# Output weights held for the second half, memory keys expanded once, unit products paced: a two-layer decoder trunk

## The chip, the cores and the metric

The kernel runs on one core of one Trainium2 chip, in one launch. The metric is the time of an execution on the device in microseconds (us). Three runs gave 2045.68, 2047.05 and 2050.27 us, so the median is 2047.05 us. The times were taken with random inputs of the sizes below.

## The reference

All is float32. The input x is 1024 tokens of width 1024. Layer 0 has a mixer of a recurrent block (width 768) beside four heads of attention over 256 memory rows, layer 1 one of sliding-window attention (12 query heads, 4 shared key/value heads, window 128) beside four heads over the same memory. After either mixer come one output projection and a SwiGLU network; each of these sits between two norms. Cut to what matters here:

```python
for l in range(2):
    hn = rms_norm(h, norm_mix_pre[l])
    mkv = rms_norm(mem, mem_norm) @ w_mem_kv[l]      # 4 heads of memory keys and values
    if l == 0:
        y = rg_lru(conv(x_r)) * gelu(gate)           # recurrent block
    else:
        y = sliding_window_attention_with_sinks(q, shared_k, shared_v, sinks)
    m_out = memory_attention(mq, mk, mv)
    mixed = concatenate([y, m_out]) @ w_out[l]       # the output projection, 1024 x 1024
    h = h + rms_norm(mixed, norm_mix_post[l])
    f = (silu(g) * u) @ w_ffn_out[l]                 # g, u = rms_norm(h, norm_ffn_pre[l]) @ w_ffn_in[l]
    h = h + rms_norm(f, norm_ffn_post[l])
```

## The kernel before, in words

Activations lie with the 1024 features on partitions, as 8 tiles of 128 (`KT`), and the tokens in two halves of 512 (`H`). Every float32 operand is split into a high and a low part (`split`, L87: a cast on ScalarE for the high one, L88, and a subtraction on VectorE for the low one, L89). A product is then three matmuls, low by high, high by high and high by low (`proj`, L148 to L150; names `al`, `ah` are the activation's parts, `wh`, `wl` the weight's). One output tile of 128 features for 512 tokens is 8 x 3 = 24 such matmuls, called a group here.

**The output projection** (`mix_out`) makes the 8 output tiles m0 to m7 for the first half, and then for the second. Its weights have two buffers (`wh`, `wl`, two of each, of 512 KB). In layer 0 the first half loads each weight, splits it, and stores m0 to m5 to DRAM (`keep`, `kept_wo`); m6 and m7 stay in the two buffers, and the second half begins with them and fetches m0 to m5 again (`fetch`, L191). In layer 1 all weights come from DRAM already split. Each output tile is copied from PSUM by ScalarE (L485) and squared and summed for the norm; for the last tile of a half the square (L490) goes by itself into `sq`. A matmul with `ones` (L233) sums `s` and `sq` over the partitions, and one with `ident` (L245) spreads the result.

**Layer 1's attention** is cut into 32 units, each a head for half the tokens: 4 memory heads (`mem_unit`, L378 to L399) and 12 window heads (`swa_unit`, L1063 to L1093) per half. A unit is a front part (scores on TensorE, maximum on VectorE, exponential on ScalarE, scaling on GpSimd) and a back part (transposes, casts, products with the values, and `acc`, L357). `attend` records the front of a unit and then the back of the one before it; it keeps the back's products in `outs`. The units are recorded between the 12 projection steps of each half (keys, values and six groups `wb`), by a table (`QUOTA`), and what is left of them between the output tiles of `mix_out`. There `place` fixes where the backs stand on TensorE: it makes the 48 matmuls that follow a chosen position wait in program order for a given product. A scheduler orders the rest within each engine. Each engine runs its instructions in that order, so one that waits holds all behind it.

The memory keys of layer 1 lie in DRAM (`kv1`). `mem_expand` splits them (`mkh`, `mkl`, L298 and L300), once for each of two pairs of heads in each half: four times in all. The loads, the stores and the fetches are issued on SyncE's queue.

Of the kernel before, what the change touches and what calls it, by code (L numbers as in the profile page):

```python
# [7 lines left out]
F32 = mybir.dt.float32  # L8
F32R = mybir.dt.float32r
# [4 lines left out]
P = 128  # L14
D = 1024
T = 1024
H = 512
KT = D // P
# [10 lines left out]
KSPLIT = 4  # L29
PLACED = 48  # L30
A_PLACES, F_PLACES, END_PLACES = (36, 54), (10, 20, 100, 110), (30, 48)
MIX_TAIL, MIX_PLACES = 2, (10, 20, 108, 118)
QUOTA = [0] * 8 + [1] * 4, [1] * 8 + [2] * 4
WEIGHT_LEAD, EVICT_LEAD, NORM_LEAD = 1000, 300, 300
NEXT_WEIGHTS = ([("wb", NL), ("wb", NL + 1), ("wk", 0), ("wk", 1), ("wv", 0), ("wv", 1)] +
                [("wb", j) for j in range(NL)] + [("wo", m) for m in range(KT)])
# [8 lines left out]
class Trunk:  # L45
# [39 lines left out]
        return self.tile(self.ap, 16, "ah", (P, H), F32R), self.tile(self.ap, 16, "al", (P, H), F32R)  # L85

    def split(self, hi, lo, src, eng=None):  # L87
        self.nc.scalar.copy(hi, src)  # L88
        return (eng or self.nc.vector).tensor_tensor(lo, src, hi.bitcast(F32), op=ALU.subtract)  # L89

    def table(self, *args, **kw):
# [389 lines left out]
    def mix_half(self, layer, act, order, steps, f, s):  # L481
        for i, (m, w) in steps:
            ps = self.proj(w(m), [act], 0, ks=order)
            f[m] = self.acc_tile()
            self.nc.scalar.copy(f[m], ps)  # L485
            if i < KT - 1:
                self.sumsq(s[0], f[m], i == 0)
            else:
                s.append(self.t("sq"))
                self.nc.scalar.activation(s[1], f[m], AF.Square)  # L490

    def mix_out(self, layer, y, order, src, early, ld):
        f, s, act = ([None] * KT, [None] * KT), [None, None], [None, None]
        hx = self.dp.tile([D, T], F32, name=f"hx{layer}")
        held, room = [], self.where["wh"][1]

        def new(m):
            if layer:
                w = self.fetch(("wo", m))
            else:  # L500
# [3 lines left out]
            held.append(w)  # L504
# [9 lines left out]
        a1 = [None] * KT  # L514
        s[0] = [self.t("s")]
        us = list(early)
        self.outs, self.mms = [], []
        for m in range(KT):
            for _ in range(-(-len(us) // max(KT - MIX_TAIL - m, 1))):
                self.attend(us.pop(0))  # L520
            if m == KT - MIX_TAIL:
                self.attend()
            done = [order[m]] if not early else order if m == KT - MIX_TAIL else []
            self.mix_split(y, 1, done, a1)
            self.mix_half(layer, a0, order, [(m, (m, new))], f[0], s[0])
        for i, g in enumerate(self.outs):
            self.place(self.mms, [[g]], [(i + 1) * len(self.mms) // (len(self.outs) + 1)])
        s[1] = [self.t("s")]
        steps = [(m, lambda m: held[m]) for m in range(KT - room, KT)]
        steps += [(m, lambda m: self.fetch(("wo", m))) for m in range(KT - room)]  # L530
        steps = list(enumerate(steps))
        self.mms = []
        self.mix_half(layer, a1, order, steps[:room], f[1], s[1])
        self.marks = []
        finish(0, self.rstd(s[0], "p")[1], ld, "s", "rsn")
        marks = self.marks
        self.mix_half(layer, a1, order, steps[room:], f[1], s[1])
# [225 lines left out]
    def ffn(self, layer, x, act, hx, finish, dst, final):  # L763
        nc = self.nc
# [97 lines left out]
        if not final:  # L862
            total(3, [(c12, c12)], ps)
            steps = order[5] + order[3]
            h0 = self.ffn_post(f0, rs, 0, gpost, r0, dst, [steps[12 * i] for i in POST_STEPS])
            for x, y in zip(c22, part):
                nc.vector.tensor_tensor(x, x, y, op=ALU.add)
            for i, g in zip(END_PLACES, marks):
                self.after(steps[i], g[-1])

            def fin():
                s = self.t("s")
                for k in range(KT):
                    self.sumsq(s, f1[k], k == 0, tag="sp")
# [47 lines left out]
    def run(self):  # L922
# [4 lines left out]
        common = dict(s=2, sq=1, sp=1, ld=2, rsn=2)  # L927
# [5 lines left out]
        self.phase("a", {"mm": 3, "gt": 2, "ss": 1, "tt": 1, "oo": 1}, mix_w, common, dict(rest=1),  # L933
                   dict(xr=4, graw=1, gwh=2, gwl=2, xc=2, xh=1, xl=1, gr=2, gi=2, a2=2), att)
        spare = [("xr", (P, 3 + H)), ("gr",), ("gi",), ("a2",)]
        mix = self.mix_out(0, *self.layer_a(), a["xT"], (), spare)
# [162 lines left out]
    def layer_b(self, h0, finish):  # L1099
# [3 lines left out]
        y = [[None] * KT for _ in range(2)]  # L1103
        kk = [[None] * 2 for _ in range(4)]
        vv = [None] * 8
        self.mem_tags = 0

        def half(n, act, f, w0, done):
            acts = [act, act]
            s = self.t("s")  # L1110
            take = self.sums([(nc.vector, s)], "00000000", ("sp", "sq"))
            for k in range(KT):
                take(k, f[k])
            rc = self.rcol(s, f"n{n}")
# [43 lines left out]
            for j in range(NL):  # L1158
                y[n][j] = self.acc_tile()
                self.rope(y[n][j], self.proj(self.fetch(("wb", j)), acts, n), tab)  # L1160
                done()

        def units(n):
            us, kv = [], {}

            def mem(j, e):
                if not kv:
                    kv["f"] = [self.load(d).rearrange("p (i c) -> p i c", i=2) for d in self.kv1]
                if e == 0:
                    kv[j] = self.mem_expand(kv["f"], j)  # L1170
                return self.mem_unit(y[n][NL + j], e, kv[j], y[n][NL + j])

            for j in range(2):
                for e in range(2):
                    us.append(lambda j=j, e=e: mem(j, e))
# [6 lines left out]
        def step(n):  # L1182
            us, at = units(n), [0]

            def done():
                i = at[0]
                at[0] += 1
                if n == 0 and i == 9:
                    h1.extend(finish())
                if i == 3:  # L1190
                    ready.extend(us[:4])
                elif i >= 6:
                    ready.extend(us[2 * i - 8:2 * i - 6])
                for _ in range(min(QUOTA[n][i], len(ready))):
# [77 lines left out]
```

## Time and profile before

| what | value |
|---|---|
| median of three runs | 2047.05 us |
| the profiled execution's own time | 2045.31 us |
| its span, from the first to the last instruction | 2043.5 us |
| outside of the span | 1.8 us |
| mean granted TensorE clock | 0.987 |
| TensorE busy | 1978.9 us, 97% of the span |
| VectorE, ScalarE, GpSimd busy | 1411.4, 1021.7, 479.2 us |

The table is read so: TensorE is busy in almost the whole span, and the other engines are not. The share hides three things, however. A matmul that runs at half clock counts as busy all the same; idle time on TensorE is spread over many short waits; and a matmul's end is modelled, so two that follow each other overlap in the rows. Waits are therefore read from the timeline, where a row that was waited for has the idle time before it and its releaser in brackets.

### The profile page before, as it was taken

The numbers are of one execution on the slowest core, as the hardware profiler recorded it, in microseconds if no ns is written. First come the engines' busy times: TensorE is split into PE (matmuls) and PEld (weight loads), VectorE is DVE, ScalarE is ACT, GpSimd is POOL, SyncE is SP. The second block draws the span as 40 slices with busy tenths as digits, with TensorE's granted clock in tenths as the row PEclk, the third lists the DMA queues.
The fourth block names the chain that finished last, engine by engine and source line by source line (L and its number), as shares of the span: only waits on it lengthen the run. The fifth ranks groups of instructions, "written<-read, shape, count | busy, mean of one in ns | idle before, by whom it ended". The sixth has DMA issues, their size and how long they took to land.

```text
span 2043.5 us, 27804 instructions
## 1 busy us (share of the span) xinstructions
PE 1978.9 (97%) x9368; PEld 1639.0 (80%) x9368; DVE 1411.4 (69%) x2313; ACT 1021.7 (50%) x1953; POOL 479.2 (23%) x476
## 2 busy tenths in 40 slices
PE   7999999999999999999999989999999999999997
PEld 6787877888888887888787877888888888888887
DVE  7877856787667676445878888678755655764566
ACT  6757774344444444445535677644433333344551
POOL 4323420014344231000034442200232323300001
PEclk9999999999999999999999989999999999999998
DMA  5422448137767879665545313171453453686653
GB/s 170 154 79 79 131 153 298 67 132 252 264 225 247 276 259 364 226 211 186 168 168 197 124 62 104 43 278 68 155 180 129 160 179 133 204 288 194 207 187 128
DMA packets 183552, 364.34 MB, mean 178 GB/s; under 512 B 20209, under 2 KB 25585, under 8 KB 183409
## 3 DMA queue, kind: packets, MB, share of 16 engines
q1 hardware_dynamic: 183408, 362.57, 52.7%
q8 instruction: 73, 1.20, 0.2%
q14 instruction: 71, 0.57, 0.1%
HBM read 254.48 MB, written 108.00 MB: 177 GB/s over the span
## 4 chain that ended last, share of the span: by engine, by line
PE 79%; DVE 9%; ACT 4%; issue 3%; DMA 3%; POOL 1%; SPq 0%; POOLq 0%; DVEq 0%; ACTq 0%
PE mm L622 12%; PE mm L624 12%; PE mm L623 12%; PE mm L730 6%; PE mm L731 6%; PE mm L732 6%; PE mm L148 5%; PE mm L149 5%; PE mm L150 5%; PE oo L1093 1%; PE tt L1086 1%; PE mm L601 1%; PE mm L602 1%; PE oo L233 1%; PE mm L603 1%
## 5 line engine op out<-in xcount | busy, mean ns | idle before, releaser
L88 ACT CAST ch<-wq 128x512 fp32r<-128x512 f32 x311 | 193.1, 621 | 423.0 <-PE mm L623 217.9
L89 DVE TENSOR_TENSOR cl<-wq,ch 128x512 fp32r<-128x512 f32 x311 | 230.7, 742 | 194.0 <-ACT ch L88 118.9
L148 PE MATMUL mm<-al,wh 128*128 128x512 f32 x616 | 250.8, 407 | 15.4 <-DVE al L965 7.4
L150 PE MATMUL mm<-ah,wl 128*128 128x512 f32 x616 | 248.3, 403 | 4.5 <-DVE wl L89 3.2
L622 PE MATMUL mm<-al,ch 128*128 128x512 f32 x640 | 252.4, 394 | 0.0
L624 PE MATMUL mm<-ah,cl 128*128 128x512 f32 x640 | 251.0, 392 | 0.0
L623 PE MATMUL mm<-ah,ch 128*128 128x512 f32 x640 | 250.3, 391 | 0.0
L149 PE MATMUL mm<-ah,wh 128*128 128x512 f32 x616 | 248.2, 403 | 0.0
L730 PE MATMUL mm<-tl,ch 128*128 128x512 f32 x532 | 207.7, 390 | 3.7 <-DVE tl L89 3.7
L731 PE MATMUL mm<-th,ch 128*128 128x512 f32 x532 | 207.0, 389 | 0.0
L732 PE MATMUL mm<-th,cl 128*128 128x512 f32 x532 | 205.1, 389 | 0.0
L622 PE MATMUL mm<-tl,ch 128*128 128x512 f32 x480 | 188.9, 393 | 0.9 <-DVE tl L89 0.9
L624 PE MATMUL mm<-th,cl 128*128 128x512 f32 x480 | 188.4, 393 | 0.0
L623 PE MATMUL mm<-th,ch 128*128 128x512 f32 x480 | 187.3, 390 | 0.0
L633 DVE TENSOR_TENSOR c<-c,mm 128x512 f32<-128x512 f32 x120 | 82.3, 686 | 110.7 <-PE mm L624 110.4
L148 PEld LDWEIGHTS mm<-al,wh 128*128 128x128 f32 x616 | 118.5, 192 | 43.9 <-DVE al L965 9.4
L150 PEld LDWEIGHTS mm<-ah,wl 128*128 128x128 f32 x616 | 118.6, 193 | 33.1 <-DVE wl L89 5.3
L624 PEld LDWEIGHTS mm<-ah,cl 128*128 128x128 f32 x640 | 120.1, 188 | 28.1
L623 PEld LDWEIGHTS mm<-ah,ch 128*128 128x128 f32 x640 | 120.2, 188 | 26.4
L622 PEld LDWEIGHTS mm<-al,ch 128*128 128x128 f32 x640 | 120.2, 188 | 26.0
L149 PEld LDWEIGHTS mm<-ah,wh 128*128 128x128 f32 x616 | 118.7, 193 | 23.1
L642 POOL TENSOR_TENSOR x<-wq,wq 128x512 f32<-128x512 f32 x36 | 50.1, 1391 | 329.6 <-DMA wq<-in_wi_dram 329.6
(347 smaller groups left out, 4300.1 us busy)
## 6 DMA issues: line engine op xcount, KB each, us to landing
wq<-in_wi_dram SPq DMA_DIRECT2D x168, 256.0 KB, 4.9
xz<-hd SPq DMA_DIRECT2D x154, 256.0 KB, 4.3
th<-xz SPq DMA_DIRECT2D x154, 256.0 KB, 3.6
wp<-in_wf_dram SPq DMA_DIRECT2D x112, 256.0 KB, 4.2
wz<-wp SPq DMA_DIRECT2D x88, 256.0 KB, 2.6
wq<-wz SPq DMA_DIRECT2D x56, 256.0 KB, 3.7
wraw<-in_wa_dram SPq DMA_DIRECT2D x27, 512.0 KB, 3.5
wq<-in_wf_dram SPq DMA_DIRECT2D x42, 256.0 KB, 3.8
```

What stands on the lines that cost most here:

```text
L88: self.nc.scalar.copy(hi, src)
L89: return (eng or self.nc.vector).tensor_tensor(lo, src, hi.bitcast(F32), op=ALU.subtract)
L148: self.mms += [nc.tensor.matmul(out, wh, al, start=i == 0, stop=False), nc.tensor.matmul(out, wh, ah, start=False, stop=False), nc.tensor. ...
L149: nc.tensor.matmul(out, wh, ah, start=False, stop=False),
L150: nc.tensor.matmul(out, wl, ah, start=False, stop=i == len(ks) - 1)]
L622: ins += [mm(out, wh, xl, start=start and k == 0, stop=False, skip_group_check=not start), mm(out, wh, xh, start=False, stop=False, skip_g ...
L623: mm(out, wh, xh, start=False, stop=False, skip_group_check=not start),
L624: mm(out, wl, xh, start=False, stop=k == 3, skip_group_check=not start)]
L633: add = lambda o, x, y: nc.vector.tensor_tensor(o, x, y, op=ALU.add)
L730: ins += [mm(ps[m], wh[:, m], xl[:, cs], start=start and p == 0, stop=False, skip_group_check=not start), mm(ps[m], wh[:, m], xh[:, cs], s ...
L731: mm(ps[m], wh[:, m], xh[:, cs], start=False, stop=False, skip_group_check=not start),
L732: mm(ps[m], wl[:, m], xh[:, cs], start=False, stop=p == NFB // 2 - 1, skip_group_check=not start)]
```

## The change

Five things are done, and TensorE's set of matmuls stays the same.

1. Layer 0 holds four output weights instead of two. m4 and m5 lie in the two buffers, m6 and m7 are split in halves straight into tiles of the attention (`SPARE`: `qs`, `pb`, `ph`). Only m0 to m3 go to DRAM; m2 and m3 come back in quarters of 256 KB into the same spare tiles. The second half uses m4, m5, m6, m7, m0, m1, m2, m3, with an order of contraction of its own (`LATE_ORDER`).
2. In layer 0 the casts of the second half's activations are recorded one by one, each after the copy of a tile (`self.after(self.cast, self.evict)`).
3. In both layers the second half's first 48 matmuls must follow the last one of the first half (`place(self.mms, [[last]], [0])`).
4. In layer 1 the memory keys are expanded once for both halves (`kv`), in other tiles (`kvf` in `pb`), and the second half's memory units stand between the window units (`MEM_UNITS`). The sums for the norms use one tile `sq` instead of `sp` and `sq`.
5. In layer 1 two more units lie before `mix_out` (`QUOTA`), and the last 22 backs (`PACED`) are spread evenly over the matmuls from step 5 of the second half on (`PACED_FROM`, `OUT_LAG`), instead of the last 12 over those of `mix_out` alone.

```diff
+PACED_FROM, PACED = 5, 22
+LATE_ORDER = [0, 1, 2, 3, 6, 7, 4, 5]
+SPARE = [[("qs", "qs"), ("pb", "pb")], [("pb", "pb"), ("ph", "ph")]]
-MIX_TAIL, MIX_PLACES = 2, (10, 20, 108, 118)
-QUOTA = [0] * 8 + [1] * 4, [1] * 8 + [2] * 4
+MIX_TAIL, OUT_LAG, MIX_PLACES = 2, 27, (10, 20, 108, 118)
+QUOTA, MEM_UNITS = ([0] * 8 + [1] * 4, [1] * 6 + [2] * 6), (2, 5, 8, 12)
...
-        held, room = [], self.where["wh"][1]
+        room = self.where["wh"][1] if layer else 2 + len(SPARE)
+        held = {}
...
+            else:
+                raw, w = self.t("wraw", (P, KT, P)), spare(m - KT)
+                nc.sync.dma_start(raw, self.a["wo"][layer, m])
+                for i in range(2):
+                    self.split(*w[i], raw[:, 4 * i:4 * i + 4])
...
+        def again(m):
+            if layer or m < len(SPARE):
+                return self.fetch(("wo", m))
+            w = spare(m - len(SPARE))
+            for i in range(2):
+                for x, d in zip(w[i], self.parted["wo", m]):
+                    nc.sync.dma_start(x.bitcast(F32), self.quad(d[:, i * H:i * H + H]))
...
-        self.outs, self.mms = [], []
+        if not layer:
+            self.outs, self.mms = [], []
...
-            done = [order[m]] if not early else order if m == KT - MIX_TAIL else []
-            self.mix_split(y, 1, done, a1)
+            if early and m == KT - MIX_TAIL:
+                self.mix_split(y, 1, order, a1)
             self.mix_half(layer, a0, order, [(m, (m, new))], f[0], s[0])
-        for i, g in enumerate(self.outs):
-            self.place(self.mms, [[g]], [(i + 1) * len(self.mms) // (len(self.outs) + 1)])
+            if not early:
+                self.mix_split(y, 1, [late[m]], a1)
+                if 0 < m < KT - 1:
+                    self.after(self.cast, self.evict)
+        outs = self.outs[-PACED:]
+        for i, g in enumerate(outs):
+            self.place(self.mms, [[g]], [OUT_LAG + (i + 1) * (len(self.mms) - OUT_LAG) // (len(outs) + 1)])
...
+        last = self.mms[-1]
         self.mms = []
...
+        self.place(self.mms, [[last]], [0])
...
-        self.mem_tags = 0
+        self.mem_tags = 1
...
-            us, kv = [], {}
+            us = []
...
-                    kv["f"] = [self.load(d).rearrange("p (i c) -> p i c", i=2) for d in self.kv1]
-                if e == 0:
-                    kv[j] = self.mem_expand(kv["f"], j)
+                    kv.update({i: self.mem_expand(kvf, i) for i in range(2)})
...
+                if n == 1 and i == PACED_FROM:
+                    self.mms = []
...
-                    ready.extend(us[:4])
+                    for j, u in enumerate(us[:4]):
+                        ready.insert(MEM_UNITS[j], u)
```

**TensorE at the end of layer 0's first half.** `mm_2851` and `mm_2849` are the group of m7 before and after, `mm_2881` and `mm_2883` the first group of the second half, `oo` the sums of the norm. Before:

```order
L148 MATMUL mm_2851<-al_2541,wh_2847 128x512
L149 MATMUL mm_2851<-ah_2540,wh_2847 128x512
L150 MATMUL mm_2851<-ah_2540,wl_2848 128x512
L233 MATMUL oo_2939<-ones,sq_2878 128x1 x4
L149 MATMUL mm_2881<-ah_2672,wh_2807 128x512
```

After:

```order
L151 MATMUL mm_2883<-al_2669,wh_2717 128x512
L152 MATMUL mm_2883<-ah_2668,wh_2717 128x512
L153 MATMUL mm_2883<-ah_2668,wl_2718 128x512
L151 MATMUL mm_2883<-al_2712,wh_2717 128x512
L236 MATMUL oo_3001<-ones,s_2544 128x1 x4
L236 MATMUL oo_3001<-ones,sq_2876 128x1 x4
L152 MATMUL mm_2883<-ah_2711,wh_2717 128x512
```

Before, the sum of `sq` stood right behind the last matmul of m7; after, ten matmuls of the next group stand between. In layer 1 the order there changes in the same way.

**ScalarE in the same place.** `ah` are the casts of the second half's activations, `wh` that of a weight, `acc` the copy of an output tile. Before:

```order
L356 COPY acc_1648<-oo_2504 64x512
L88 CAST ah_2586<-acc_1648 128x512
L88 CAST ah_2629<-acc_1715 128x512
L88 CAST ah_2672<-acc_1788 128x512
L88 CAST ah_2715<-acc_1942 128x512
L88 CAST ah_2758<-acc_2015 128x512
L88 CAST ah_2801<-acc_2203 128x512
L88 CAST ah_2841<-acc_2276 128x512
L88 CAST wh_2847<-wraw_2845 128x1024
L485 COPY acc_2796<-mm_2771 128x512
```

After:

```order
L488 COPY acc_2746<-mm_2721 128x512
L91 CAST ah_2751<-acc_1615 128x512
L211 ACTIVATE sq_2748<-acc_2746 128x512
L359 COPY acc_1648<-oo_2504 64x512
L488 COPY acc_2786<-mm_2761 128x512
L91 CAST ah_2791<-acc_1648 128x512
L211 ACTIVATE sq_2788<-acc_2786 128x512
L488 COPY acc_2830<-mm_2805 128x512
L91 CAST ah_2835<-acc_2203 128x512
L91 CAST ah_2878<-acc_2276 128x512
```

Seven casts stood in a row ahead of a weight's cast; now they stand singly behind copies, and no weight's cast is behind them.

**TensorE in layer 1's attention.** `mm_11906` (before) and `mm_11055` (after) are groups of the second half: `mm_11906` is the first output tile, `mm_11055` the query projection `wb1`; the rows between are products of units. Before, with the first and the last rows of a stretch of 144:

```order
L148 MATMUL mm_11906<-al_11756,wh_11902 128x512
L149 MATMUL mm_11906<-ah_11755,wh_11902 128x512
L150 MATMUL mm_11906<-ah_11755,wl_11903 128x512
L1063 MATMUL ss_11210<-kl_2068_9582,qs_11190 128x256
...
L393 MATMUL tt_11886<-ident,pb_11637 128x128 x2
L148 MATMUL mm_11906<-al_11760,wh_11902 128x512
```

After, with the first and the last rows of a stretch of 88:

```order
L151 MATMUL mm_11055<-al_10000,wh_11051 128x512
L1123 MATMUL oo_10876<-pl_10861,vv_2080_9626 128x256
...
L1123 MATMUL oo_11191<-ph_11184,vv_2086_9710 128x128
L152 MATMUL mm_11055<-ah_9999,wh_11051 128x512
```

Before, the stretch without a projection matmul held 166 matmuls of units; after, one of 103 stands earlier, and behind it 504 matmuls of units and 296 of projections alternate to the end of the first half of `mix_out`.

## Rows read from the trace of the kernel before

**Rows 1.** The page: busy time, and shares of the chain that ended last.

```profile
PE 1978.9 (97%) x9368; PEld 1639.0 (80%) x9368; DVE 1411.4 (69%) x2313; ACT 1021.7 (50%) x1953; POOL 479.2 (23%) x476
...
PE 79%; DVE 9%; ACT 4%; issue 3%; DMA 3%; POOL 1%; SPq 0%; POOLq 0%; DVEq 0%; ACTq 0%
```

**Rows 2.** Windows: us; busy of PE, PEld, DVE, ACT, POOL; clock; DMA share; GB/s.

```profile
450.00:475.00 25.00, 25.00 (x111) 20.42 (x110) 20.43 (x30) 10.15 (x18) 8.74 (x6) 1.00 0.80 282
...
306.40:309.80 3.40, 3.40 (x10) 2.67 (x9) 0.00 (x0) 0.00 (x0) 0.69 (x1) 0.50 0.00 0
330.30:337.10 6.80, 6.54 (x17) 4.88 (x18) 0.00 (x0) 1.93 (x4) 0.00 (x0) 0.50 1.04 396
```

**Rows 3.** Timeline of TensorE, layer 0's output projection: start, us, [idle before, releaser].

```profile
294.27 0.50 PE L148 MATMUL mm<-al,wh 128*128 128x512 f32 x1 [1.80 <-ACT wh L88]
...
304.74 1.05 PE L233 MATMUL oo<-ones,sq 128*128 128x1 f32 x8 [1.34 <-ACT sq L490]
...
330.56 0.77 PE L148 MATMUL mm<-al,wh 128*128 128x512 f32 x1 [2.35 <-DMA wh<-kept_wo]
...
347.53 0.47 PE L148 MATMUL mm<-al,wh 128*128 128x512 f32 x1 [0.69 <-ACT acc L485]
...
354.83 0.47 PE L148 MATMUL mm<-al,wh 128*128 128x512 f32 x1 [0.80 <-ACT ah L88]
...
362.02 0.51 PE L601 MATMUL mm<-al,th 128*128 128x512 f32 x1 [0.68 <-ACT acc L485]
```

**Rows 4.** Timeline of ScalarE, the same place.

```profile
289.52 3.75 ACT L88 CAST ah<-acc 128x512 fp32r<-128x512 f32 x7 [2.81 <-DVE acc L357]
293.17 1.04 ACT L88 CAST wh<-wraw 128x1024 fp32r<-128x1024 f32 x1
```

**Rows 5.** Timeline of SyncE's queue, the same place.

```profile
317.78 6.24 SPq L554 DMA_DIRECT2D hx<-acc  x8
324.11 0.54 SPq L191 DMA_DIRECT2D wh<-kept_wo  x1
```

**Rows 6.** Windows of layer 1's attention, second half, to the end of `mix_out`'s first half.

```profile
1158.70:1197.40 38.70, 38.70 (x234) 34.08 (x232) 31.61 (x86) 21.76 (x60) 20.19 (x27) 1.00 0.39 137
1197.40:1233.80 36.40, 28.65 (x153) 23.77 (x150) 31.97 (x80) 30.85 (x93) 13.84 (x29) 0.81 0.00 1
1233.80:1324.70 90.90, 88.31 (x528) 76.18 (x527) 66.32 (x189) 67.11 (x181) 24.05 (x48) 0.98 0.24 82
```

**Rows 7.** Windows inside the second of these.

```profile
1200.70:1207.50 6.80, 6.66 (x28) 5.52 (x28) 5.17 (x21) 5.43 (x17) 2.41 (x4) 0.50 0.00 0
...
1221.10:1224.50 3.40, 3.30 (x16) 3.24 (x16) 3.04 (x6) 2.08 (x9) 2.08 (x6) 0.51 0.00 0
```

**Rows 8.** Windows of L149 alone, a third of the projections' matmuls: PE, PEld.

```profile
1158.70:1197.40 38.70, 14.27 (x36) 6.61 (x35) 1.00 0.39 137
1197.40:1233.80 36.40, 0.00 (x0) 0.00 (x0) 0.81 0.00 1
1233.80:1324.70 90.90, 24.84 (x63) 11.90 (x63) 0.98 0.24 82
```

**Rows 9.** Windows of L357 alone, one for each unit's end: DVE.

```profile
1158.70:1197.40 38.70, 3.39 (x5) 1.00 0.39 137
1197.40:1233.80 36.40, 4.08 (x6) 0.81 0.00 1
1233.80:1324.70 90.90, 10.22 (x15) 0.98 0.24 82
```

**Rows 10.** Window before the shared keys' projection, where VectorE splits the memory queries.

```profile
1022.00:1036.00 14.00, 14.00 (x68) 11.70 (x67) 8.50 (x12) 3.68 (x6) 4.78 (x4) 1.00 0.11 47
```

**Rows 11.** Timeline of VectorE and TensorE at the second expansion of the keys.

```profile
1085.18 3.19 DVE L300 TENSOR_TENSOR mkl<-ld,mkh 64x256 fp32r<-64x256 f32 x4
...
1087.62 0.36 PE L378 MATMUL ss<-mkl,qs 128*128 128x256 f32 x1 [2.24 <-DVE mkl L300]
```

**Rows 12.** Timeline of TensorE, layer 1's end of the first half of `mix_out`.

```profile
1326.23 1.23 PE L233 MATMUL oo<-ones,sq 128*128 128x1 f32 x8 [0.55 <-ACT sq L490]
```

More of the change, by code (lines that the diff above doesn't have):

```diff
@@ L87, in split @@
     def split(self, hi, lo, src, eng=None):
-        self.nc.scalar.copy(hi, src)
+        self.cast = self.nc.scalar.copy(hi, src)
         return (eng or self.nc.vector).tensor_tensor(lo, src, hi.bitcast(F32), op=ALU.subtract)
@@ L484, in mix_half @@
             f[m] = self.acc_tile()
-            self.nc.scalar.copy(f[m], ps)
+            self.evict = self.nc.scalar.copy(f[m], ps)
             if i < KT - 1:
@@ L492, in mix_out @@
     def mix_out(self, layer, y, order, src, early, ld):
+        nc = self.nc
         f, s, act = ([None] * KT, [None] * KT), [None, None], [None, None]
         hx = self.dp.tile([D, T], F32, name=f"hx{layer}")
-        held, room = [], self.where["wh"][1]
+        room = self.where["wh"][1] if layer else 2 + len(SPARE)
+        held = {}
         def new(m):
@@ L499, in new @@
                 w = self.fetch(("wo", m))
-            else:
+            elif m < KT - len(SPARE):
                 w = self.weight(self.a["wo"][layer, m])
@@ L503, in new, with spare @@
                     self.keep(("wo", m), w)
-            held.append(w)
+            else:
[3 more added lines that the diff above has]
+                    self.split(*w[i], raw[:, 4 * i:4 * i + 4])
+            held[m] = w
+            return w
+        def spare(i):
+            return [[self.quad(self.t(tag, dt=F32R)) for tag in tags] for tags in SPARE[i]]
+        def again(m):
[5 more added lines that the diff above has]
+                    nc.sync.dma_start(x.bitcast(F32), self.quad(d[:, i * H:i * H + H]))
             return w
@@ L513, in mix_out @@
         a0 = self.mix_split(y, 0, order)
-        a1 = [None] * KT
+        a1, late = [None] * KT, order if layer else LATE_ORDER
         s[0] = [self.t("s")]
         us = list(early)
-        self.outs, self.mms = [], []
+        if not layer:
+            self.outs, self.mms = [], []
         for m in range(KT):
@@ L522, in mix_out @@
                 self.attend()
-            done = [order[m]] if not early else order if m == KT - MIX_TAIL else []
-            self.mix_split(y, 1, done, a1)
+            if early and m == KT - MIX_TAIL:
+                self.mix_split(y, 1, order, a1)
             self.mix_half(layer, a0, order, [(m, (m, new))], f[0], s[0])
-        for i, g in enumerate(self.outs):
-            self.place(self.mms, [[g]], [(i + 1) * len(self.mms) // (len(self.outs) + 1)])
+            if not early:
[5 more added lines that the diff above has]
+            self.place(self.mms, [[g]], [OUT_LAG + (i + 1) * (len(self.mms) - OUT_LAG) // (len(outs) + 1)])
         s[1] = [self.t("s")]
         steps = [(m, lambda m: held[m]) for m in range(KT - room, KT)]
-        steps += [(m, lambda m: self.fetch(("wo", m))) for m in range(KT - room)]
+        steps += [(m, again) for m in range(KT - room)]
         steps = list(enumerate(steps))
+        last = self.mms[-1]
         self.mms = []
-        self.mix_half(layer, a1, order, steps[:room], f[1], s[1])
+        self.mix_half(layer, a1, late, steps[:room], f[1], s[1])
         self.marks = []
@@ L536, in mix_out @@
         marks = self.marks
-        self.mix_half(layer, a1, order, steps[room:], f[1], s[1])
+        self.mix_half(layer, a1, late, steps[room:], f[1], s[1])
+        self.place(self.mms, [[last]], [0])
         for i, g in zip(MIX_PLACES, marks):
@@ L873, in fin @@
                 for k in range(KT):
-                    self.sumsq(s, f1[k], k == 0, tag="sp")
+                    self.sumsq(s, f1[k], k == 0)
                 rs1 = self.rstd(s, "p")[1]
@@ L926, in run @@
         self.kv1 = [self.dp.tile([P, H], F32, name=f"mkv1_{i}") for i in range(2)]
-        common = dict(s=2, sq=1, sp=1, ld=2, rsn=2)
+        common = dict(s=2, sq=1, rsn=2)
         att = dict(qs=2, pb=4, ph=2, pl=2, nm=6, sm=6, es=6)
@@ L932, in run @@
                dict(wq=6, wp=4), quad(2), quad(3), quad(1))
[L933 removed]
+        self.phase("a", {"mm": 3, "gt": 2, "ss": 1, "tt": 1, "oo": 1}, mix_w, {**common, "sp": 1}, dict(rest=1),
                    dict(xr=4, graw=1, gwh=2, gwl=2, xc=2, xh=1, xl=1, gr=2, gi=2, a2=2), att)
@@ L1110, in half @@
             s = self.t("s")
-            take = self.sums([(nc.vector, s)], "00000000", ("sp", "sq"))
+            take = self.sums([(nc.vector, s)], "00000000", ("sq",))
             for k in range(KT):
@@ L1161, in half @@
                 done()
+        kvf = [self.load(d, "pb").rearrange("p (i c) -> p i c", i=2) for d in self.kv1]
+        kv = {}
         def units(n):
-            us, kv = [], {}
+            us = []
             def mem(j, e):
                 if not kv:
-                    kv["f"] = [self.load(d).rearrange("p (i c) -> p i c", i=2) for d in self.kv1]
-                if e == 0:
-                    kv[j] = self.mem_expand(kv["f"], j)
+                    kv.update({i: self.mem_expand(kvf, i) for i in range(2)})
                 return self.mem_unit(y[n][NL + j], e, kv[j], y[n][NL + j])
```

## The prediction, made before the changed kernel ran

> **What bounds the kernel now.** I read the page first. TensorE is busy in 97% of the span and takes 79% of the chain that ended last; the next engine, VectorE, is at 69% and 9% [rows 1]. So the time is TensorE's. Its set of matmuls is the same after the change, and what can be won is only its idle time and the time at half clock.
>
> Next I read the windows, to see what a matmul costs when nothing is waited for. 111 matmuls of 512 columns fill 25.00 us, which is 0.225 us each [rows 2]. The small matmuls of the attention units have a price of their own. In the first window of [rows 6] TensorE has no idle time; of its 234 matmuls 36 x 3 = 108 are projections [rows 8], so the 126 of units took 38.7 - 108 x 0.225 = 14.4 us, 0.114 us each. (From the order I count 106 and 128, which gives 0.116; I use 0.113, the start-to-start distance that units show where they run on without a wait.)
>
> With these two prices the three windows of [rows 6] can be held against their contents. I count matmuls in the order, since a few records are missing from the trace. The first loses about 0.4 us. The second holds 166 matmuls of units and no projection [rows 8]: 36.4 us against 166 x 0.113 = 18.8, so 17.6 us are lost, and a matmul costs 0.219 us there. The third holds 338 of units and 190 of projections: 90.9 - 38.2 - 42.8 = 9.9 us lost. Together they lose 28 of 166.0 us. The second window shows why: without projections between, units wait for each other's steps on VectorE and ScalarE (31.97 and 30.85 us busy of 36.4), and the clock falls to a mean of 0.81 [rows 6].
>
> Last I read the timeline where the change acts. Layer 0's projection has single waits and two stretches at half clock [rows 2, 3]; layer 1 has a wait for memory keys and one at the end of `mix_out`'s first half [rows 11, 12].
>
> **The change part by part: layer 0.** All of these waits lie on TensorE, so each counts in full.
>
> - 1.80 us for a weight's cast [rows 3]. It stood behind seven casts in a row, which took 3.75 us [rows 4]. After the change no weight's cast is behind them: gone.
> - 1.34 us for the square of the last tile [rows 3], followed by 3.4 us at clock 0.50 [rows 2], which costs half of that, 1.7 us. Ten matmuls, 2.25 us, now stand between m7's last and the sums. The copy and the square were done 1.34 us after TensorE had come to them, so 2.25 us cover them.
> - 2.35 us for a weight that was fetched late [rows 3]. Its fetch was issued at 324.11, behind eight stores that had held the queue for 6.24 us [rows 5], and 6.4 us ahead of the matmul. The stretch at half clock behind it lasts 6.8 us [rows 2] and costs 3.4. With four weights held, the first fetched weight is needed 4 x 24 x 0.225 = 21.6 us after the half begins instead of 10.8, and 4 MB are fetched in place of 6 MB (each weight is two tensors of 512 KB). What is late next would be the fetch of m2 and m3 into the spare tiles, which waits for m6's and m7's last use, but these are needed four groups later, some 21 us, against the 6.4 us of [rows 5].
> - 0.69 and 0.80 us at the fifth and sixth fetched weights [rows 3] and two waits of about half a us behind them, 2.5 us in all. These weights were fetched into a buffer that was just released; the last two of the new order have been on the way for far longer.
>
> The sum is 1.80 + 3.04 + 5.75 + 2.47 = 13.1 us.
>
> Two costs come against it. The feed-forward network's first weights are kept in tiles that overlay the spare ones. So the casts of its first weights now wait for the last matmuls of m2 and m3, and ScalarE's later casts stand behind them in its queue. Before, this seam cost 0.68 us [rows 3]. I can't see the new wait in this trace. At the least it is nothing; at the most it is a whole chain of a cast, a subtraction and the evictions queued with them, some 10 us if everything that stood on ScalarE in the 3.75 us row [rows 4] came twice or more. I take 2.5 us, near the two waits of that row's kind (1.80 and 2.81), and 0.9 us more, half of a short half-clock stretch [rows 2], since long ones followed waits of 1.34 and 2.35 us. Layer 0 is then worth 13.1 - 3.4 = 9.7 us; from 13.1 down to 3.
>
> **Layer 1, the keys.** The wait of 2.24 us for `mkl` [rows 11] goes, and with it a stretch of 3.4 us at clock 0.50 behind it (three stretches of this length bear on the sum, and one of them stands in [rows 2]): 2.24 + 1.7 = 3.9 us. The two expansions move to where VectorE is busy for 8.50 of 14 us and TensorE has projections of its own [rows 10]; they cost about 3 us each on VectorE [rows 11] and fit, though the shared values behind them may come 0.5 us later. I take 3.4 us, from 1 to 3.9.
>
> **Layer 1, the end.** The ten matmuls cover the square here as well: 0.55 us [rows 12] and a half-clock stretch of 3.4 us, 1.7 us, together 2.2.
>
> **Layer 1, the pacing.** This is the largest term and the least certain. The stretch without a projection is not gone: the order leaves 103 matmuls of units alone, now ahead of the first paced position, at the second query projection. At the price of [rows 6] they lose 103 x (0.219 - 0.113) = 10.9 us instead of 17.6. Behind it 504 matmuls of units and 296 of projections alternate, 123.6 us by the two prices. Nothing lost in them would be like the first window of [rows 6], with 0.83 projections to a unit's matmul; 0.029 us lost at each unit's matmul, like the third, with 0.56, would be 14.8 us. The ratio here is 296 / 504 = 0.59, at the lower end, but the third window was unevenly filled. Another row gives a bound: in the second and the third window a unit ended every 36.4 / 6 = 6.07 and 90.9 / 15 = 6.06 us [rows 9], with and without projections. If that is the units' own pace, 21 paced ones take 127.3 us and 3.7 us are lost. I take 9 us, the middle of 3.7 and 14.8. The loss is 10.9 + 9 = 20 us instead of 28: 8 us gained, between 0 and 17 (14.8 lost and 2 of late first backs at one end, none at the other).
>
> The half clock is part of the price of those 103 matmuls. The row shows it at a mean of 0.81, though no wait in the window was longer than a wait that left the clock alone elsewhere (1.80 us at 294.27 [rows 3]); of the 36.4 us 13.6 were at 0.50, two of the three stretches are in [rows 7], and they cost 6.8 us. The Trainium skill has two rules for this. "TensorE: Matmul & The Clock Gate", section "HAM oscillation — how this bites in real kernels", has the clock fall after long waits for DMA between bursts; by that the new stretch keeps its clock and loses 103 x (29.6 / 166 - 0.113) = 6.7 us instead of 10.9, and the forecast would be 4 us lower. Its section "A second HAM failure mode: psum-queue depth-cycling" has frequent short waits do the same; by that the price stays. The trace agrees with the second, at 0.81.
>
> **The sum.** 9.7 + 3.4 + 2.2 + 8 = 23.3 us. From the profiled execution's 2045.31 us this gives 2022.0. The median of the runs shown is 1.7 us above that execution, so I predict 2024 us.
>
> **The rivals.**
>
> 1. The paced stretch runs as the first window of [rows 6], with nothing lost, and the seam in layer 0 costs nothing. Then layer 0 gives 13.1, the keys 3.9, the end 2.2, the pacing 28 - 10.9 = 17.1: 36.3 us, 2011 us. For it: an even ratio of projections, and VectorE needs only (31.61 + 31.97 + 66.32) / 26 = 5.0 us for a unit [rows 6, 9]. Against it: the pace of 6.07 us.
> 2. The loss only moves. The 103 matmuls and 14.8 us behind them leave the pacing a gain of 2.3, and the seam in layer 0 takes 10: 3.1 + 1 + 2.2 + 2.3 = 8.6 less some late backs, 2038 to 2043 us.
> 3. Slower: the pacing itself holds TensorE. A projection matmul behind a post can't run until the back of its unit has, and that back waits for exponential, scaling, cast and subtraction on the other engines. If units come slower than posts, each post is an idle TensorE. The 103 matmuls take 22.6 us, and with T us to a unit the stretch takes 22.6 + 21 T, against 163 us for the same matmuls before (166.0 less 25 matmuls of units). The other gains are 15.3 us, so it decides from T = (163 + 15.3 - 22.6) / 21 = 7.4 us. At 7.7 us, as in the first window (5 units in 38.7 us [rows 9]), it is 6 us slower, 2053 us. For it: that window. Against it: there TensorE was never idle [rows 6], so its own work set that pace, and 6.07 us was reached twice.
> 4. The change doesn't do what it says: the first posts come too late to fill the stretch they are meant for. The order shows just that for 103 matmuls, and the forecast has their price in it.
>
> **How the numbers follow.** The forecast, with a gain of 14 to 32 us, has 0.60; rival 1 has 0.17, rival 2 0.14, the slower one 0.09. What this kernel's measurement can tell from no change is about 0.2%, 4 us. Half of rival 2 lies inside that. Faster is then 0.60 + 0.17 + 0.07 = 0.84, the same 0.07, slower 0.09. The range goes from 2009 (rival 1 with 2 us more from the clock) to 2041, in the middle of rival 2; outside it lie 0.07 and 0.09 above, and some 0.03 below.
>
> **What would show it.** Layer 0: no wait over 1 us on TensorE from 285 us on up to the network's first weight, and there a new one for a cast. Fewer and later fetches of `kept_wo`. Layer 1: no wait for `mkl` after the first; `sq` not waited for. A window with no projections should stand at the second query projection, of some 22 us, with a clock below 0.9, and behind it a unit's end every 6.1 to 6.4 us. The forecast is wrong if units end every 7 us or more there, with TensorE idle at the backs' products; if the network's start shows more than 5 us of waits; or if the clock falls in the paced stretch.

## The result, and the profile after

The changed kernel took 2032.01 us in the median of four runs (2029.64 to 2039.25), beside 2046.92 us before in the same comparison: ratio 0.9931, with an interval of 0.9903 to 0.9958, or 15 us less. Forecast were 23 us less, 2024 us, in a range of 2009 to 2041. The sign and the range held; the size did not come from where I had put it.

The profiled run of the changed kernel is its slowest, 2039.25 us with a span of 2037.5 us. So its parts are read one by one, and its whole is not. The page, busy time and the chain that ended last, answers to [rows 1] and hardly differs from it:

```profile
PE 1977.2 (97%) x9368; PEld 1640.0 (80%) x9368; DVE 1408.1 (69%) x2303; ACT 1017.8 (50%) x1943; POOL 483.9 (24%) x476
...
PE 78%; DVE 11%; ACT 4%; issue 3%; DMA 3%; POOL 1%; SPq 0%; POOLq 0%; DVEq 0%; ACTq 0%
```

Two waits that no part of the change touches serve as marks, since they stand in every trace: TensorE waits 0.46 us for `x` in either feed-forward network, and 1.5 us for `tl` near the end of the first. Between the second mark and the third lies layer 1's mixer. The timeline of TensorE at the three marks, before (start, us, idle time before):

```profile
388.37 1.05 PE L233 MATMUL oo<-ones,x 128*128 128x1 f32 x8 [0.46 <-DVE x L223]
...
989.61 0.50 PE L730 MATMUL mm<-tl,ch 128*128 128x512 f32 x1 [1.46 <-DVE tl L89]
...
1399.44 1.05 PE L233 MATMUL oo<-ones,x 128*128 128x1 f32 x8 [0.46 <-DVE x L223]
```

And after:

```profile
379.58 1.05 PE L236 MATMUL oo<-ones,x 128*128 128x1 f32 x8 [0.46 <-DVE x L226]
...
983.69 0.50 PE L760 MATMUL mm<-tl,ch 128*128 128x512 f32 x1 [1.51 <-DVE tl L92]
...
1392.08 1.05 PE L236 MATMUL oo<-ones,x 128*128 128x1 f32 x8 [0.46 <-DVE x L226]
```

Layer 0 ends 8.8 us earlier. Layer 1's mixer took 1399.44 - 989.61 = 409.8 us and now takes 408.4: 1.4 us less (3.4 in a second profile, below), where 13.6 were forecast. The windows of the changed kernel show the places (us; busy of PE, PEld, DVE, ACT, POOL; clock; DMA share; GB/s):

```profile
285.00:345.00 60.00, 60.00 (x283) 49.72 (x282) 41.26 (x62) 28.86 (x51) 4.95 (x4) 1.00 0.59 212
...
349.60:359.80 10.20, 10.20 (x34) 8.65 (x33) 3.42 (x7) 2.56 (x5) 1.01 (x1) 0.50 0.37 113
1134.30:1142.20 7.90, 5.50 (x30) 5.10 (x30) 7.73 (x21) 6.93 (x19) 0.00 (x0) 0.78 0.11 27
1154.56:1175.78 21.22, 18.17 (x104) 15.01 (x103) 16.95 (x50) 15.20 (x43) 10.14 (x18) 0.84 0.02 7
1175.78:1315.60 139.82, 132.52 (x795) 113.52 (x795) 107.87 (x296) 99.08 (x274) 50.51 (x86) 0.99 0.27 91
```

In the first window, layer 0's projection, TensorE is never idle and at full clock: the waits of [rows 3] and both stretches at half clock of [rows 2] are gone. The fourth and fifth answer to [rows 6]: the run of 103 unit matmuls alone takes 21.22 us (22.6 were forecast), and the paced stretch behind it 139.82 us (132.6 were forecast). The third is new. The timeline of TensorE at the new waits:

```profile
348.47 0.50 PE L631 MATMUL mm<-al,th 128*128 128x512 f32 x1 [2.51 <-ACT acc L488]
...
1081.69 0.38 PE L381 MATMUL ss<-mkl,qs 128*128 128x256 f32 x1 [0.91 <-ACT pb L95]
1088.67 0.39 PE L381 MATMUL ss<-mkl,qs 128*128 128x256 f32 x1 [1.14 <-ACT pb L95]
...
1137.69 0.39 PE L1175 MATMUL mm<-wh,al 128*128 128x256 f32 x1 [1.43 <-DVE ah L349]
```

The first is the seam to the feed-forward network: 2.51 us, with 10.2 us at clock 0.50 behind it. The next two stand where the wait for `mkl` [rows 11] was, and come from the exponentials of the memory units' scores. The last is a wait for the split of a value, in the third window above, where the clock falls too.

### The profile page after: what moved, and what is told of

Its sections match the earlier page's. It is cut to its first block, busy times and chain, and to the rows that moved or that the text cites. A ratio compares the mean times of both kernels' runs of the same rounds, so it can differ in the third digit from the quotient of the medians.

```text
span 2037.5 us, 27767 instructions
## 1 busy us (share of the span) xinstructions
PE 1977.2 (97%) x9368; PEld 1640.0 (80%) x9368; DVE 1408.1 (69%) x2303; ACT 1017.8 (50%) x1943; POOL 483.9 (24%) x476
## 4 chain that ended last, share of the span: by engine, by line
PE 78%; DVE 11%; ACT 4%; issue 3%; DMA 3%; POOL 1%; SPq 0%; POOLq 0%; DVEq 0%; ACTq 0%
PE mm L652 12%; PE mm L654 12%; PE mm L653 12%; PE mm L760 6%; PE mm L762 6%; PE mm L761 6%; PE mm L153 5%; PE mm L151 5%; PE mm L152 5%; PE oo L1123 1%; DVE al L92 1%; PE oo L236 1%; DVE tl L92 1%; PE mm L632 1%; PE tt L1116 1%
## 5 line engine op out<-in xcount | busy, mean ns | idle before, releaser
L151 PE MATMUL mm<-al,wh 128*128 128x512 f32 x568 | 229.7, 404 | 10.6 <-DVE al L995 8.3
L153 PE MATMUL mm<-ah,wl 128*128 128x512 f32 x568 | 227.7, 401 | 4.2 <-DVE wl L92 4.0
L152 PE MATMUL mm<-ah,wh 128*128 128x512 f32 x568 | 227.3, 400 | 0.0
L151 PEld LDWEIGHTS mm<-al,wh 128*128 128x128 f32 x568 | 108.5, 191 | 35.3 <-DVE al L995 10.4
L153 PEld LDWEIGHTS mm<-ah,wl 128*128 128x128 f32 x568 | 108.4, 191 | 28.8 <-DVE wl L92 6.0
L152 PEld LDWEIGHTS mm<-ah,wh 128*128 128x128 f32 x568 | 108.6, 191 | 21.2
```

The source lines that it names most:

```text
L151: self.mms += [nc.tensor.matmul(out, wh, al, start=i == 0, stop=False), nc.tensor.matmul(out, wh, ah, start=False, stop=False), nc.tensor. ...
L152: nc.tensor.matmul(out, wh, ah, start=False, stop=False),
L153: nc.tensor.matmul(out, wl, ah, start=False, stop=i == len(ks) - 1)]
```

## The experiments

Each kernel was timed beside the kernel before, in three groups, in which that kernel's median was 2046.6, 2048.2 and 2046.6 us. The table has the median, and from each profile the end of layer 0 (the first mark) and layer 1's mixer (the third less the second); "changed" has its first profile and the one taken again.

| kernel | median, us | first mark | layer 1's mixer |
|---|---|---|---|
| before | 2046.6 | 388.4 | 409.8 |
| changed; again | 2032.0; 2032.1 | 379.6; 376.4 | 408.4; 406.4 |
| layer 0 alone | 2034.9 | 375.2 | 408.0 (old) |
| layer 1 alone | 2048.1 | 389.1 (old) | 409.7 |
| seam | 2032.0 | 372.8 | 407.6 |
| 27 paced | 2033.7 | 379.1 | 405.8 |
| seam, 27 paced | 2031.1 | 373.7 | 408.9 |
| seam, old layer 1 | 2030.5 | 376.7 | 407.7 (old) |
| memory units in front | 2027.0 | 375.8 | 399.4 |
| memory units in a row | 2033.1 | 374.9 | 411.4 |
| three in front | 2027.3 | 377.3 | 402.3 |
| seam, three in front | 2023.1 | 372.1 | 399.6 |
| the same, 27 paced | 2026.8 | 373.0 | 405.1 |

**Layer 0's part alone** (before, with `SPARE`, `LATE_ORDER`, single casts; `place` of `last` in layer 0 only).

```diff
...
+        if not layer:
+            self.place(self.mms, [[last]], [0])
...
```

> The kernel before with layer 0's part of the change alone (four held weights, casts one by one, second half behind the last matmul). Theory A (the terms of the forecast hold, and layer 0 carries most of the gain): 9 to 11 us less than before, ratio about 0.995; no wait on TensorE from 290 to 345 us; at the network's start one wait of about 2.5 us and a clock of 0.50 for some 10 us behind it. Rival B (the gain of the whole change comes from layer 1, and layer 0's gain is eaten at the network's start): less than 5 us.

Measured: ratio 0.995 (0.9937 to 0.9964), 11.7 us less. Theory A holds, but for the half clock behind the wait; the gain is a little over its 9 to 11 us. The wait at the seam, by this kernel's timeline of TensorE, and the window behind it:

```profile
348.88 0.50 PE L629 MATMUL mm<-al,th 128*128 128x512 f32 x1 [2.51 <-ACT acc L487]
```

```profile
349.00:359.20 10.20, 10.20 (x57) 8.86 (x58) 5.47 (x10) 4.16 (x8) 1.01 (x1) 1.00 0.45 148
```

The wait is the same 2.51 us, and here the clock stays at 1.00 behind it. Whether the clock falls there is not fixed by the order of instructions.

**Layer 1's part alone** (the changed kernel, with layer 0's projection as before).

```diff
-        room = self.where["wh"][1] if layer else 2 + len(SPARE)
+        room = self.where["wh"][1]
...
-        self.place(self.mms, [[last]], [0])
+        if layer:
+            self.place(self.mms, [[last]], [0])
```

The rest of the edit takes the spare tiles and the single casts out of layer 0.

> The changed kernel with layer 0's output projection as it was before, so layer 1's part alone (keys expanded once, alternating memory units, pacing, second half behind the last matmul). Theory A: 2 to 6 us less than before, ratio 0.997 to 0.999, because the stretch of unit matmuls without projections is only moved (103 of them instead of 166, 21 us in one piece) and the waits of the first half's keys come back as shorter ones. Rival B: 10 us or more less, ratio 0.995 or below.

Measured: ratio 1.0008 (0.9996 to 1.0019). Not even the 2 us of theory A are there, and rival B is out: layer 1's part is worth nothing by itself.

**Seam.**

```diff
...
+        if not layer:
+            first, rest = [6, 7, 4, 5], [2, 3, 0, 1]
...
```

> The changed kernel with one thing moved: layer 0's second half takes its tiles in the order m6, m7, m4, m5, m2, m3, m0, m1, so that the spare tiles are released two groups (11 us) before the feed-forward network's first casts, which overlay them. Theory A (the wait of 2.51 us at the network's start and the 10.2 us at clock 0.50 behind it come from those casts): both go, 5 to 8 us less than the changed kernel, about 2025 us. Rival C (the wait there comes from the evictions and the weights' DMA, whatever tiles are used): the wait stays at 2 us or more, time as the changed kernel within 2 us.

Measured: 2032.02 us, ratio 0.9935 (0.9923 to 0.9948). Its timeline and window at the seam:

```profile
346.50 0.50 PE L634 MATMUL mm<-al,th 128*128 128x512 f32 x1 [0.79 <-ACT acc L488]
```

```profile
346.60:356.80 10.20, 10.20 (x57) 8.85 (x58) 3.32 (x7) 1.10 (x2) 1.01 (x1) 1.00 0.01 3
```

The changed kernel's timeline of ScalarE at the seam shows what the copy (L488) stood behind: four casts of the network's first weights, and these waited 2.65 us for a matmul:

```profile
345.76 2.18 ACT L91 CAST th<-wq 128x512 fp32r<-128x512 f32 x4 [2.65 <-PE mm L152]
347.85 0.57 ACT L488 COPY acc<-mm 128x512 f32<-128x512 f32 x1
```

The mechanism is shown: with the tiles free two groups earlier the wait is 0.79 us, near the 0.68 of before [rows 3], and the first mark comes at 372.8 us. In the five profiles with this order the wait is 0.79 to 1.05 us, and the clock stays at 1.00 behind it. The time is no lower than the changed kernel's, which only rival C had; here the 1.7 us, and the clock where it would have fallen, don't stand out from the spread of the runs. (With other units in front, below, the medians with and without the seam order lie 4 us apart.)

**27 paced backs.**

```diff
-PACED_FROM, PACED = 5, 22
+PACED_FROM, PACED = 5, 27
-MIX_TAIL, OUT_LAG, MIX_PLACES = 2, 27, (10, 20, 108, 118)
+MIX_TAIL, OUT_LAG, MIX_PLACES = 2, 0, (10, 20, 108, 118)
```

> The changed kernel with 27 paced backs instead of 22, from the first matmul on (OUT_LAG 0 instead of 27). In the order of TensorE the longest run of unit matmuls without a projection is then 36 or so instead of 103. Theory A (the unfilled run is what layer 1 still loses): the stretch of 21 us at 0.206 us a matmul is gone, 6 to 10 us less than the changed kernel, about 2023 us. Rival D (the units' own pace of some 6 us is the limit, so that the loss is spread over the paced stretch): within 3 us of the changed kernel, and units still end every 6 us or so with short waits on TensorE all along. Rival E (more posts hold TensorE): slower than the changed kernel.

Measured: 2033.69 us, ratio 0.9946 (0.9934 to 0.9959). The run of 103 matmuls is gone from the order, and nothing is won: theory A falls, rival D stands. As it has it, units still end every 6.0 us (27 in 163 us of this profile, by L360), with short waits on TensorE between.

**The changed kernel again** (no edit).

> The changed kernel once more, beside the three below. About 2032 us, 14 to 15 us less than before. Its profile shows which half-clock stretches come back and which were chance: theory A has the wait of 2.5 us at the network's start and the run of 103 unit matmuls (20 to 22 us) in every profile; the stretch at 0.50 behind the wait may be missing, as it was with layer 0's part alone.

Measured: 2032.14 us, ratio 0.9924 (0.991 to 0.9937). Its window behind the seam has a clock of 0.83, between the two above (0.50 and 1.00):

```profile
349.00:359.20 10.20, 10.20 (x52) 8.75 (x51) 4.05 (x7) 3.81 (x8) 1.01 (x1) 0.83 0.40 132
...
1148.22:1168.02 19.80, 15.65 (x104) 12.50 (x103) 16.27 (x49) 15.00 (x43) 10.11 (x18) 1.00 0.03 14
```

The second row is the run of 103 unit matmuls. Here it has the full clock, and still takes 19.80 us where 103 x 0.113 = 11.6 would do. So most of the loss in it, 8.2 of the first profile's 9.6 us, is not the clock's.

**Seam and 27 paced** (both edits).

> The seam order of layer 0 (m6, m7, m4, m5, m2, m3, m0, m1) and 27 paced backs from the first matmul on, together. Theory A': the seam gives 2 to 7 us against the changed kernel in the same call and the pacing 0 to 3, so 2025 to 2030 us. Theory D (unit pace is the limit, half-clock stretches come by chance): within 3 us of the changed kernel.

Measured: 2031.07 us, ratio 0.9921 (0.9908 to 0.9934). Within 3 us of the changed kernel, as theory D has it; theory A', 2030 us at the most, is missed by 1 us.

**Memory units in front.**

```diff
-QUOTA, MEM_UNITS = ([0] * 8 + [1] * 4, [1] * 6 + [2] * 6), (2, 5, 8, 12)
+QUOTA, MEM_UNITS = ([0] * 8 + [1] * 4, [1] * 6 + [2] * 6), (0, 1, 2, 3)
```

> The changed kernel with the second half's four memory units in a row again (MEM_UNITS 0, 1, 2, 3), everything else kept. Theory F (the new wait of 1.43 us for a value's split at 1136 us comes from window units, which put four mask instructions of 0.48 us each on VectorE ahead of it): that wait falls to 0.3 us or is gone, the loss of TensorE in that place falls from 5 us to about 1.5, as before the change, and the run of unit matmuls (92) stays: 3 us less than the changed kernel or less. Rival G (the values are late whatever unit stands there): the wait stays at 1.4 us.

In this kernel the first half's output projection reads the tile of the last window unit before that unit's result is in it; all instructions run, but that one dependence is missing. Measured: 2027.04 us, ratio 0.99 (0.9886 to 0.9915). The wait at the values is gone, so theory F is right on the place, and the gain, 5 us, is more than it allowed.

**Old layer 1 with the seam order** (keys, units and pacing as before; `last` in both layers).

> Layer 0's part of the change with the seam order, and of layer 1's part only the rule that the second half's first matmuls of the output projection follow the first half's last. Keys, memory units and pacing of layer 1 are as before the change. Theory A'' (layer 1's pacing, keys and order of units are worth nothing in sum): within 3 us of the seam run, 2030 to 2034 us, and the wait for the square (0.55 us) is gone. Rival B' (they are worth the 5 us or more that the whole change shows over layer 0's part alone): 2035 us or more.

Measured: 2030.45 us, ratio 0.9919 (0.9906 to 0.9933). Theory A'' holds: without the new keys, alternation and pacing the time is that of the changed kernel, within the intervals.

**Three memory units in front, the fourth behind the window units** (every dependence kept).

```diff
-QUOTA, MEM_UNITS = ([0] * 8 + [1] * 4, [1] * 6 + [2] * 6), (2, 5, 8, 12)
+QUOTA, MEM_UNITS = ([0] * 8 + [1] * 4, [1] * 6 + [2] * 6), (0, 1, 2, 12)
```

> The changed kernel with three of the second half's memory units at the head of the queue and the fourth behind the first half's window units (MEM_UNITS 0, 1, 2, 12). Theory F (window units at the values' steps put their mask instructions and the keys' splits ahead of the values' split on VectorE): no wait of 1.4 us at the values' matmuls, loss of TensorE there 2.5 us instead of 5, no half-clock stretch behind it; 2 to 6 us less than the changed kernel's 2032. Rival G' (the gain of the run with all four in front came from the head whose result the output projection didn't wait for): 2030 us or more.

Measured: 2027.28 us, ratio 0.9908 (0.9896 to 0.9921), 4.8 us less than the changed kernel, and 5.8 less than the next kernel below, which was timed in the same group and whose interval lies apart. Rival G' is out. The cause of the wait is on VectorE. Its timeline in the changed kernel, ahead of the values' split (L349; L303 splits the shared keys, and L1095 adds the mask to a window unit's scores and takes their maximum):

```profile
1133.21 1.56 DVE L303 TENSOR_TENSOR al<-kf,ah 64x512 fp32r<-64x512 f32 x2
1134.80 0.48 DVE L1095 CUSTOM_DVE_ANT_0 pb<-ss,mask,cst 128x256 f32<-128x256 f32 x1
...
1135.21 0.48 DVE L1095 CUSTOM_DVE_ANT_0 pb<-ss,mask,cst 128x256 f32<-128x256 f32 x1
...
1135.73 1.39 DVE L303 TENSOR_TENSOR al<-kf,ah 64x512 fp32r<-64x512 f32 x2
1137.15 0.48 DVE L349 SCALAR_TENSOR_TENSOR ah<-mm,rcn,ah 128x256 fp32r<-128x256 f32 x1
```

And with three memory units in front:

```profile
1123.04 1.58 DVE L303 TENSOR_TENSOR al<-kf,ah 64x512 fp32r<-64x512 f32 x2 [0.25 <-ACT ah L301]
1124.65 0.48 DVE L349 SCALAR_TENSOR_TENSOR ah<-mm,rcn,ah 128x256 fp32r<-128x256 f32 x1
1125.05 1.28 DVE L383 TENSOR_REDUCE nm<-ss 128x2 f32<-128x512 f32 x2
```

The window of its values' matmuls:

```profile
1120.00:1132.00 12.00, 12.00 (x98) 11.65 (x97) 10.93 (x22) 11.37 (x32) 7.88 (x12) 1.00 0.32 106
```

With a window unit there, two mask instructions and the second pair of key splits stand ahead of the values' split, and TensorE waits 1.43 us for it and then runs at a clock of 0.78. With a memory unit the split comes right behind the keys, and the maximum of the scores after it: TensorE is not idle for 12 us, at full clock.

**Memory units in a row behind the window units.**

```diff
-QUOTA, MEM_UNITS = ([0] * 8 + [1] * 4, [1] * 6 + [2] * 6), (2, 5, 8, 12)
+QUOTA, MEM_UNITS = ([0] * 8 + [1] * 4, [1] * 6 + [2] * 6), (90, 91, 92, 93)
```

> The changed kernel with the second half's memory units in a row behind the first half's window units, as before the change (pacing, keys and all else kept). Theory F: the wait at the values stays or is near that of before (window units stand at the values' steps in both), so no gain at that place; what remains of the alternation is the paced stretch, where four memory units in a row lean on ScalarE and GpSimd: within 3 us of the changed kernel. Rival H (alternating is what loses): 3 us or more less than the changed kernel.

Measured: 2033.11 us, ratio 0.9937 (0.9924 to 0.995). The 1.43 us stay. Alternating the memory units neither wins nor loses; rival H is out. By these two runs what pays is which unit stands at the values; what the same edit does to the stretches behind them was not separated from it.

**Seam order and three in front.**

> Seam order of layer 0 and MEM_UNITS 0, 1, 2, 12 together. If both gains are real and independent: 1.7 us (the shorter wait at the network's start, more where the clock would have fallen there) below the run with the memory units alone, 2023 to 2028 us, the fastest so far.

Measured: 2023.05 us, ratio 0.9887 (0.9871 to 0.9902): 23.6 us less than before, 9 less than the changed kernel. This version beats both. Its interval overlaps that of three in front alone (0.9896 to 0.9921), so that the seam order adds its 4 us is likely and not certain.

**The same with 27 paced.**

> The same with 27 paced backs from the first matmul on, so that no run of unit matmuls is longer than 36. Theory A: the 99 unit matmuls without projections still cost 7 to 9 us there, so 2018 to 2024 us. Theory D (the loss goes to the paced stretch, whatever the run is): within 3 us of the run without it.

Measured: 2026.75 us, ratio 0.9907 (0.9894 to 0.9919), 3.7 us more than without. Theory A falls a second time: to take the run of unit matmuls apart wins nothing. By the medians it costs a little more than theory D allows, but the intervals overlap.

## Why the prediction was right or wrong

**Layer 0: right.** Forecast 9.7 us, alone 11.7. All waits of [rows 3] ahead of the seam went, as did the fall of the clock behind two of them. The seam's wait was sized at 2.5 us and is 2.51, by the mechanism named: ScalarE's copy of an output tile stood behind casts that waited for the spare tiles, and the seam order takes it away. The half clock behind it was put at 0.9 us. Of seven traces that have this wait two show it for 10.2 us, which costs 5.1 us, two for about 3.4 us, and three not at all: 1.9 us in the mean.

**The keys: the step failed.** "The wait of 2.24 us for `mkl` goes" is right, but I did not ask what is late next. The scores now wait for the exponentials of scores before them, 0.91 and 1.14 us in the first profile and up to 1.5 in others; that the expansion had hidden these is my reading, which no run tests. The shared values come 0.25 us later, as was allowed for. The timeline of TensorE at their first wait, before:

```profile
1050.86 0.39 PE L1145 MATMUL mm<-wh,al 128*128 128x256 f32 x1 [1.54 <-DVE vv L346]
```

And after, with the window behind it:

```profile
1045.11 0.38 PE L1175 MATMUL mm<-wh,al 128*128 128x256 f32 x1 [1.79 <-DVE vv L349]
```

```profile
1045.90:1049.30 3.40, 3.40 (x19) 3.40 (x18) 3.34 (x7) 0.00 (x0) 0.00 (x0) 0.51 0.34 77
```

So these waits sum to 3.8 us before (1.54 + 2.24) and 3.8 after (1.79 + 0.91 + 1.14). The fall of the clock behind `mkl`, 1.7 us, went, and one of the same length came behind the shared values: in this profile nothing of the 3.4 us is left. The new fall stands in three of the eleven profiles with the new keys, so 1.2 us are left in the mean.

**The end: right.** The wait for the square is gone from both layers. Of its 2.2 us in layer 1, the 1.7 for the clock are not sure: with layer 0's part alone the 0.55 us stayed there, and the clock did not fall behind them.

**The pacing: the step failed twice.** The price of the run of 103 nearly held, 9.6 us lost where 10.9 were forecast, though the clock's part was 1.4 us by the two profiles, and not 4. The first failure is the size of the paced stretch. I took 9 us of loss, between the pace of 6.07 us a unit and the third window's price of 0.029 us a unit's matmul. The stretch took 139.82 us for a content of 123.6: 16.2 lost, 0.032 each, at the bad end. These windows of L360, which adds up a unit's result, count the units' ends in it:

```profile
1154.56:1175.78 21.22, 2.71 (x4) 0.84 0.02 7
1175.78:1315.60 139.82, 14.98 (x22) 0.99 0.27 91
```

That is 6.4 us a unit, at the end of the 6.1 to 6.4 named as a sign, and not the 6.07 on which the better end of the sum rested. A sign of being wrong came too, the clock in the paced stretch: it fell once, for 3.4 us, as this window shows.

```profile
1223.60:1227.00 3.40, 3.40 (x9) 2.62 (x9) 1.84 (x4) 3.22 (x11) 0.00 (x0) 0.52 0.02 5
```

Second, I left out what the new order of units does ahead of the pacing. One unit's mask instructions at the values' steps cost the 1.43 us and the clock behind it: the clock falls there in all seven profiles with this wait (1.43 or 1.44 us), and in none of the four with memory units in front. In sum 9.6 us lost in the run of 103, 16.2 in the paced stretch and some 4 at the values are 30, against 28 before and 1.2 at the values.

**Where the reason, not the size, was wrong.** I took the run without projections for the loss itself. With 27 paced backs there is no such run, and the time stays or rises. So the loss is not where projections are lacking; it goes wherever the units' steps on the other engines end late. That fits rival 3's mechanism at a milder price, and not rival 1. That the units' own steps set the pace was not tried by making one of them shorter; it stays the reading that is left. And memory units in front win 4 to 9 us in layer 1 by the table (1 to 4 with 27 paced), where 4 were lost at the values. The rows tell in part what gives the rest. In layer 1's mixer the seven profiles with the wait of 1.43 us have in the mean 17.2 us of idle time on TensorE, and 7.5 lost to half clock (an estimate: half of the time at 0.50); the four with memory units in front have 15.6 and 2.1. So most of the 6.7 us between their mean times is clock that did not fall, at the values and behind them; why it holds better behind them is open.

The Trainium skill has the clock fall where TensorE idles briefly and often ("TensorE: Matmul & The Clock Gate", section "A second HAM failure mode: psum-queue depth-cycling"). The run of 103 agrees in the first profile, with a clock of 0.84 though none of its waits is over 0.72 us. In the second profile its waits are as short, 0.73 us at the most, and the clock stays at 1.00.

## What to carry to other kernels

A stretch in which TensorE lacks filler is a symptom; before filler is moved there, ask which engine ends the waits in it, and price the moved work at the worst window that looks like it. When a wait goes, look for the next releaser in the same place. When units change places, list what each puts on the engine that a third party waits for: here the choice of three units was worth 5 us, more than all the rest of layer 1's part.

## What the runs showed of the hardware

Whether the clock falls behind a wait can differ from one execution to the next. The same wait of 2.51 us was followed by 10.2 us at 0.50, by a mean of 0.83, or by 1.00. The four runs of the changed kernel lie 9.6 us apart, with mean clocks of 0.987 (2039.25 us), 0.991 twice and 0.994 (2029.64 us). In the first profile the clock also fell far from the change; the timeline and the window there:

```profile
788.81 0.50 PE L760 MATMUL mm<-tl,ch 128*128 128x512 f32 x1 [2.31 <-DVE tl L92]
```

```profile
789.90:793.30 3.40, 3.40 (x10) 2.62 (x9) 2.90 (x5) 1.47 (x4) 0.00 (x0) 0.51 1.05 402
```

The kernel before waited 1.00 us there and kept its clock. Nor does a fall cost the same everywhere: at a clock of 0.84 the run of 103 took 21.22 us and at 1.00 19.80, which is 1.4 us less, though half of its time at 0.50 is 3.4. So one profile of this kernel tells where time goes to some 5 us, and a gain of that size needs several runs.
